# First token tiles ahead of the first two weight tiles in a hybrid encoder layer

## The chip, the cores and the metric

The kernel runs on one core of a Trainium2 chip. The time is that of one execution on the device, in microseconds; the median of several runs is given, and one further execution was taken by the hardware profiler.

## What is computed

One layer of a bidirectional encoder on 1024 tokens of width 1024, in float32. The reference, cut to its steps:

```python
h = rms_norm(x, g_mix_pre)
proj = h @ w_in                       # 1024 x 2832
aq, ak, av, dqkv, dgate, dalpha, dbeta = split(proj)
attn_o = window_attention(rope(aq), rope(ak), av, sink)          # 8 heads, +-128 tokens
dn_o = gated_deltanet(dqkv, dgate, dalpha, dbeta, conv_w, ...)   # 4 heads, both directions
x = x + rms_norm(concat(attn_o, dn_o) @ w_out, g_mix_post)
c = cross_attention(rms_norm(x, g_cross_pre), rms_norm(mem, g_mem), w_cq, w_ckv, w_co)
x = x + rms_norm(c, g_cross_post)
f = (silu(hn @ w_gate) * (hn @ w_up)) @ w_down                   # hn = rms_norm(x, g_ffn_pre)
return x + rms_norm(f, g_ffn_post)
```

The DeltaNet part sends its q, k and v columns through a short convolution of five taps, then solves small triangular systems for chunks of tokens and carries a state along the sequence in both directions.

## The kernel before

Tokens are handled in tiles of 128 (eight tiles, `NT`), the width in eight slices of 128 (`KT`). A large product is made from three: each operand is split into a high part (a rounding cast on ScalarE, line 102) and a low part (the difference, line 103), and high x high, high x low and low x high are added up in PSUM. `split` does both steps. The low part is taken on VectorE unless another engine is named.

`load_w` (line 118) fetches a weight tile of 128 columns, 512 KB, with a DMA from SyncE (line 122) and splits it into `whi` and `wlo`. Its pool `wp` holds two raw tiles (`wraw`) and two of each part, so the third weight tile is loaded when the first raw tile has been split.

The start of the kernel brings the tokens in. For each of the eight token tiles: a DMA of 512 KB into `xt`; ScalarE squares it and sums up (line 214, `junk`, `ss`); GpSimd makes the factor from the sum (`rstd_of`, lines 157 and 158, `rs`); VectorE multiplies by this factor and by the gain `gmix` (line 217); TensorE turns the tile by eight 128x128 transposes against `ident` (line 222); and `split` makes `hhi` and `hlo` of each half of it. The tiles stand in a ring of six buffers (`bufs=6`). Four tiles make one half of the sequence, `hT[0]` or `hT[1]`, and a product needs a whole half.

The first products (line 292) are those of head 0's k and q columns: two weight tiles, `ws`, against both halves. Their results go through `conv` (lines 269 to 281): ScalarE copies them out of PSUM, VectorE does four taps (line 279).

Then follow ORDER_1 (the other DeltaNet projections, `prep`, the inverse of the small blocks), ORDER_2 (gates, the further levels of the inverse, value, key and query projections of the attention, and first windows `W`) and ORDER_3, the scan stage:

```python
ORDER_3 = ("M " + "s01 W K " * 5 + "s01 K K K K " * 2 + "s01 K s01 K K").split()
```

`M` normalises the memory tokens, `s01` is one step of the two scans, which load `kv` and `pz` (lines 765 and 766) and do small products (line 757); `W` works on two windows of the attention, which load `vr`, `kr` and `qr` (lines 604 to 607), make scores (line 627), turn the weights (line 650), split them into `ph` and `pl` and multiply by the values (line 655); `K` makes one column tile of the memory's keys or values (lines 885 to 896). At the end, `ol` is normalised (line 832) and turned (line 837), and the mixer's output `d_mix` is read back in `mraw` and split into `b` for the product with `w_out` (line 976). After that come the cross-attention and the FFN.

The order of the instructions on each engine is not that of the source. A planner simulates the whole program's course and puts each engine's instructions in a queue by their due times and priorities; `tc.high_priority(AHEAD)` moves a weight's loading and splitting ahead. Each engine then works through its queue in order. All DMAs are issued from SyncE's queue.

In the program before, the loads stand on SyncE in this order: the two weight tiles, `ident`, the first token tile, `gmix`, five more token tiles, then small tables with the third and fourth weight tiles between them, then the last two token tiles. On VectorE both `wlo` stand ahead of the first line 217.

Of the kernel before, what the change touches and what calls it, by code (L numbers as in the profile page):

```python
# [10 lines left out]
F32 = mybir.dt.float32  # L11
# [8 lines left out]
P = 128  # L20
S = 1024
D = 1024
KT = D // P
# [52 lines left out]
def tile_hybrid_block(  # L76
# [4 lines left out]
    g_ffn_pre, w_gate_up, w_down, g_ffn_post, consts, out, dump=None, stop=None,  # L81
):
    nc = tc.nc
    x, mem, out = x[0], mem[0], out[0]
# [3 lines left out]
    if dump is None:  # L88
        def dump(name, ap):
            pass  # L90
# [8 lines left out]
    def split(hi, lo, src, scale=None, eng=None):  # L99

        if scale is None:
            nc.scalar.copy(hi, src)  # L102
            (eng or nc.vector).tensor_tensor(lo, src, f32(hi), ALU.subtract)  # L103
        else:
            nc.scalar.activation(hi, src, AF.Identity, scale=scale)
            nc.vector.scalar_tensor_tensor(lo, src, scale, f32(hi), ALU.mult, ALU.subtract)

    def pool(name, bufs, **kw):
        return tc.tile_pool(name=name, bufs=bufs, reuse_waits="tile", **kw)
# [5 lines left out]
    dram = ctx.enter_context(tc.tile_pool(name="dram", bufs=1, space=DRAM))  # L115
    wp = ctx.enter_context(pool("wp", 2))

    def load_w(src, k, n, eng=None):

        with tc.high_priority(AHEAD):  # L120
            raw = wp.tile([P, k, n], F32, tag="wraw", name="wraw")
            nc.sync.dma_start(raw, src.rearrange("(k p) n -> p k n", p=P))
            hi = wp.tile([P, k, n], F32R, tag="whi", name="whi")
            lo = wp.tile([P, k, n], F32R, tag="wlo", name="wlo")
            split(hi, lo, raw, eng=eng)
        return hi, lo


    ident = cst.tile([P, P], F32, name="ident")
    nc.sync.dma_start(ident, consts[:, 0:P])  # L130
    mhalf = cst.tile([P, 16], F32, name="mhalf")
    nc.gpsimd.memset(mhalf, -0.5)
    cols = cst.tile([P, P], F32, name="cols")
# [20 lines left out]
    def rstd_of(rs, ss, n, eps):  # L154

        w = ss.shape[-1]
        nc.gpsimd.tensor_scalar(rs, ss, n, eps, ALU.mult, ALU.add)
        nc.gpsimd.tensor_tensor(rs, rs, mhalf[:, :w], ALU.pow)  # L158
# [34 lines left out]
    t1 = pa1.enter_context(pool("t1a", 2, side="right"))  # L193

    def small():
        return ps.tile([P, 512], F32, tag="ps", name="ps")


    xts = [t1.tile([P, D], F32, tag="xt", name="xt", bufs=6) for _ in range(2)]
    nc.sync.dma_start(xts[0], x[0:P, :])  # L200
    gmix = t1.tile([P, D], F32, tag="gmix", name="gmix", bufs=1)
    nc.sync.dma_start(gmix, g_mix_pre[0].partition_broadcast(P))
    hT = []
    for hf in range(2):
        hi = hx.tile([P, KT, HALF], F32R, name=f"hhi{hf}")
        lo = hx.tile([P, KT, HALF], F32R, name=f"hlo{hf}")
        for j in range(4):
            t = 4 * hf + j
            xt = xts[t] if t < 2 else t1.tile([P, D], F32, tag="xt", name="xt", bufs=6)
            if t:  # L210
                nc.sync.dma_start(xt, x[t * P:(t + 1) * P, :])
            junk = t1.tile([P, D], F32, tag="junk", name="junk", bufs=1)
            ss = t1.tile([P, 1], F32, tag="ss", name="ss", bufs=4)
            nc.scalar.activation(junk, xt, AF.Square, accum_out=ss)
            rs = t1.tile([P, 1], F32, tag="rs", name="rs", bufs=4)
            rstd_of(rs, ss, 1.0 / D, EPS)
            nc.vector.scalar_tensor_tensor(xt, xt, rs, gmix, ALU.mult, ALU.mult)
            for kq in range(2):
                pt = small()
                for k in range(4):  # L220
                    c = (4 * kq + k) * P
                    nc.tensor.transpose(pt[:, k * P:(k + 1) * P], xt[:, c:c + P], ident)
                o = slice(4 * kq, 4 * kq + 4), slice(j * P, (j + 1) * P)
                split(hi[:, o[0], o[1]], lo[:, o[0], o[1]], pt.rearrange("p (k t) -> p k t", k=4))
        hT.append((hi, lo))
        dump(f"hT{hf}", (hi, lo))
# [30 lines left out]
    def proj(src_cols, eng=None):  # L257
        whi, wlo = load_w(src_cols, KT, P, eng)
        pp = [pg.tile([P, 512], F32, tag="pg", name="pg") for _ in range(2)]
        gemm_b(whi, wlo, hT, pp)  # L260
        return pp
# [21 lines left out]
    def dcols(i, h):  # L283
        return w_in[:, 768 + (4 * i + h) * P:768 + (4 * i + h + 1) * P]


    ws = [load_w(dcols(i, 0), KT, P) for i in (1, 0)]
    pps = [[None, None], [None, None]]
    for hf in range(2):
        for i in range(2):  # L290
# [4 lines left out]
    t1 = pa1.enter_context(pool("t1b", 1, side="right"))  # L295
# [581 lines left out]
    def next_kv():  # L877

        ct = kv_done[0]
        kv_done[0] += 1  # L880
        whi, wlo = load_w(w_ckv[:, ct * P:(ct + 1) * P], KT, P, nc.gpsimd)
        pp = pc.tile([P, 512], F32, tag="pc", name="pck")[:, 0:ML]
        for k in range(KT):
            for i, (w, a) in enumerate(((whi, 0), (whi, 1), (wlo, 0))):
                nc.tensor.matmul(pp, w[:, k, :], mT[a][:, k, :], start=(k == 0 and i == 0), stop=(k == KT - 1 and i == 2))
        cv = mk.tile([P, ML], F32, tag="cv", name="cv", bufs=2)
        nc.scalar.copy(cv, pp)
        if ct < KT:
            nc.sync.dma_start(d_mk[ct * P:(ct + 1) * P, :], cv)
            return  # L890
        pt = pc.tile([P, 512], F32, tag="pc", name="ptv")[:, 0:ML]
        for t in range(2):
            nc.tensor.transpose(pt[:, t * P:(t + 1) * P], cv[:, t * P:(t + 1) * P], ident)
        vv = mk.tile([P, 2, P], F32, tag="vv", name="vv", bufs=2)
        nc.scalar.copy(vv, pt.rearrange("p (t n) -> p t n", t=2))
        nc.sync.dma_start(d_mv[:, :, (ct - KT) * P:(ct - KT + 1) * P].rearrange("t p n -> p t n"), vv)
# [116 lines left out]
    for hf in range(2):  # L1013
        for kp in range(4):
            k2 = slice(2 * kp, 2 * kp + 2)
            raw = raw01 if hf == 0 and kp < 2 else raws[hf]
# [83 lines left out]
    raw = tr.tile([P, KT, HALF], F32, name="xraw")  # L1100
# [24 lines left out]
    for k in range(HK):  # L1125
        p0, p1 = turned_k(xn, k), turned_k(xn, k + HK)
        g0, g1 = gain("ffn", k), gain("ffn", k + HK)
        x12, t1, t2_, t3_ = (tr.tile([P, HALF], F32, name=f"r{i}", tag=f"r{i}") for i in range(4))
# [57 lines left out]
    ws = LA.enter_context(pool("ws", 2, side="right"))  # L1186
# [179 lines left out]
```

## Time and profile before

| | |
|---|---|
| median of 3 runs | 1670.23 us (1670.08 to 1673.58) |
| profiled execution | 1670.74 us |
| its span, first to last instruction | 1669.0 us |
| mean granted clock of TensorE | 0.975 |
| TensorE busy | 1569.7 us, 94% of the span |
| VectorE, ScalarE, GpSimd busy | 926.9, 752.5, 655.2 us |

The profile has one row for an engine, a line of the kernel and an operation: when it started, how long it took, what it wrote and read, and in brackets how long the engine had sat idle before it and what ended that. PE is TensorE's matmul side and PEld its weight loads, DVE is VectorE, ACT ScalarE, POOL GpSimd, SP SyncE, SPq its queue of DMAs. A row of the windows gives the length of a stretch, the busy time of PE, PEld, DVE, ACT and POOL with their counts, the granted share of TensorE's clock, the share of time that the DMA engines were busy, and GB/s. A row of the waits gives who waited for whom, the total in us, how often, and the longest.

### The profile page before, as it was taken

Reading aid. Unit: us, or ns where it says so; the run is one execution under the profiler, and the core shown is the slowest. Engines: PE = TensorE matmul, PEld = TensorE weight load, DVE = VectorE, ACT = ScalarE, POOL = GpSimd, SP = SyncE. Lnnn points to the kernel's source line nnn. Section 1 sums busy time; section 2 is a strip of 40 time slices with the busy share of each in tenths; the row PEclk is TensorE's granted clock in tenths of the full one; section 3 lists DMA queues with packets and bytes.
Section 4 is the critical chain, followed back from the end, with each engine's and each line's share of the span. In section 5 each row is a group of like instructions: output and inputs, shape, how many; then the busy total and the mean of one; then the engine's idle time right before and its main releaser. Section 6 shows DMA issues by size and latency. Waiting matters only on the chain.

```text
span 1669.0 us, 21742 instructions
## 1 busy us (share of the span) xinstructions
PE 1569.7 (94%) x7802; PEld 1314.5 (79%) x7802; DVE 926.9 (56%) x1407; ACT 752.5 (45%) x1528; POOL 655.2 (39%) x557
## 2 busy tenths in 40 slices
PE   6989889997999879899999999999999999999998
PEld 5878778886888767678888777788888888888886
DVE  6754987876776543453335348677544554335342
ACT  6555553246867754554335555233323332445221
POOL 2467552344437534664225340334333332321010
PEclk9999999897999999999999999999999999999999
DMA  5134256665998456354222164343222223566452
GB/s 197 40 113 139 85 164 174 164 172 159 322 313 268 111 161 235 126 177 151 76 64 99 60 208 134 119 126 102 76 76 82 88 92 105 192 203 209 137 166 77
DMA packets 275560, 240.49 MB, mean 144 GB/s; under 512 B 43240, under 2 KB 226941, under 8 KB 275453
## 3 DMA queue, kind: packets, MB, share of 16 engines
q1 hardware_dynamic: 275453, 239.11, 46.0%
q8 instruction: 61, 1.00, 0.3%
q14 instruction: 46, 0.38, 0.1%
HBM read 177.69 MB, written 58.75 MB: 142 GB/s over the span
## 4 chain that ended last, share of the span: by engine, by line
PE 53%; POOL 3%; DMA 2%; DVE 2%; issue 2%; ACT 1%; SPq 0%; POOLq 0%; ACTq 0%
PE pd L1320 7%; PE pd L1295 7%; PE pD L1149 7%; PE pE L1149 7%; PE pA L1149 7%; PE pmg L976 6%; PE pcq L254 5%; PE pB L1149 3%; PE pco L1084 1%; PE pcs L1058 1%; POOL wlo L103 1%; DMA d_mv<-vv 1%; DMA mraw<-d_mix 1%; POOL prs L158 0%; POOL pr L158 0%
## 5 line engine op out<-in xcount | busy, mean ns | idle before, releaser
L103 POOL TENSOR_TENSOR wlo<-wraw,whi 128x1024 fp32r<-128x1024 f32 x88 | 217.5, 2473 | 294.8 <-ACT whi L102 281.5
L102 ACT CAST whi<-wraw 128x1024 fp32r<-128x1024 f32 x108 | 113.4, 1050 | 170.1 <-issue 74.9
L254 PE MATMUL pg<-hhi,whi 128*128 128x512 f32 x352 | 143.2, 408 | 0.0
L254 PE MATMUL pg<-hhi,wlo 128*128 128x512 f32 x352 | 142.1, 404 | 0.0
L254 PE MATMUL pg<-hlo,whi 128*128 128x512 f32 x352 | 142.1, 404 | 0.0
L976 PE MATMUL pmg<-whi,b 128*128 128x512 f32 x384 | 117.1, 400 | 7.4 <-ACT whi L102 5.2
L1149 PE MATMUL pA<-b,whi 128*128 128x512 f32 x352 | 111.2, 398 | 3.6 <-ACT m L1166 3.1
L279 DVE SCALAR_TENSOR_TENSOR acc<-cp,cols,acc 128x1024 f32<-128x1024 f32 x48 | 77.4, 1614 | 35.0 <-ACT acc L277 34.3
L1226 POOL TENSOR_TENSOR act<-act,up 128x512 f32<-128x512 f32 x33 | 47.8, 1449 | 114.5 <-issue 63.1
L976 PEld LDWEIGHTS pmg<-whi,b 128*128 128x128 f32 x384 | 73.3, 193 | 23.7 <-ACT whi L102 5.6
L1149 PEld LDWEIGHTS pA<-b,whi 128*128 128x128 f32 x352 | 66.4, 191 | 18.6 <-ACT m L1166 4.4
L254 PEld LDWEIGHTS pg<-hhi,wlo 128*128 128x128 f32 x352 | 68.4, 194 | 13.8
L254 PEld LDWEIGHTS pg<-hhi,whi 128*128 128x128 f32 x352 | 68.4, 195 | 13.5 <-ACT hhi L102 0.2
L254 PEld LDWEIGHTS pg<-hlo,whi 128*128 128x128 f32 x352 | 68.3, 194 | 13.4
L1198 POOL TENSOR_TENSOR sr<-wraw 128x512 f32<-128x512 f32 x22 | 28.5, 1297 | 115.9 <-DMA wraw<-in_w_gate_up_dram 107.3
L976 PE MATMUL pmg<-wlo,b 128*128 128x512 f32 x192 | 70.1, 395 | 1.3 <-POOL wlo L103 1.3
L1149 PE MATMUL pA<-b,wlo 128*128 128x512 f32 x176 | 69.6, 397 | 0.0
L1320 PE MATMUL pd<-wdh,ath 128*128 128x512 f32 x176 | 69.5, 395 | 0.0
L1320 PE MATMUL pd<-wdh,atl 128*128 128x512 f32 x176 | 69.5, 395 | 0.0
L1320 PE MATMUL pd<-wdl,ath 128*128 128x512 f32 x176 | 69.5, 395 | 0.0
L1295 PE MATMUL pd<-dl,whi 128*128 128x512 f32 x176 | 68.5, 389 | 0.0
L1295 PE MATMUL pd<-dh,wlo 128*128 128x512 f32 x176 | 68.4, 389 | 0.0
(392 smaller groups left out, 4222.1 us busy)
## 6 DMA issues: line engine op xcount, KB each, us to landing
wraw<-in_w_gate_up_dram SPq DMA_DIRECT2D x52, 512.0 KB, 4.0
kv<-d_kv SPq DMA_DIRECT2D x32, 512.0 KB, 6.2
wraw<-in_w_in_dram SPq DMA_DIRECT2D x22, 512.0 KB, 4.1
araw<-d_act SPq DMA_DIRECT2D x22, 512.0 KB, 3.4
draw<-in_w_down_dram SPq DMA_DIRECT2D x22, 512.0 KB, 4.4
atr<-d_act SPq DMA_DIRECT2D x16, 704.0 KB, 4.7
d_act<-act SPq DMA_DIRECT2D x40, 256.0 KB, 2.7
d_kv<-kv SPq DMA_DIRECT2D x8, 1024.0 KB, 6.3
```

Source lines behind the costliest of these rows:

```text
L102: nc.scalar.copy(hi, src)
L103: (eng or nc.vector).tensor_tensor(lo, src, f32(hi), ALU.subtract)
L254: nc.tensor.matmul(p_, w[:, k, :], ah[a][:, k, :], start=(k == 0 and i == 0), stop=(k == nk - 1 and i == 2))
L279: nc.vector.scalar_tensor_tensor(acc, cp[:, t:t + S], taps[t], acc, ALU.mult, ALU.add)
L976: nc.tensor.matmul(pp[t], act[a][:, k, tt], w_[:, kk, :], start=(k == 0 and i == 0), stop=(k == KT - 1 and i == 2))
L1058: nc.tensor.matmul(pp[:, t2_, :], q[a][:, ct, tt], kr_[b_][:, ct, :], start=(j == 0 and i == 0), stop=(j == 1 and i == 2))
L1084: nc.tensor.matmul(po, vr_[a][:, kt, cs], pts[kt][b_], start=(kt == 0 and i == 0), stop=(kt == 1 and i == 2))
L1149: nc.tensor.matmul(out_, w[a][:, k, :], xx[b_][:, k, :], start=(start and k == 0 and i == 0), stop=(k == HK - 1 and i == 2), skip_group_ch ...
L1198: nc.gpsimd.tensor_tensor(s[0], b_[:, 0:HK], b_[:, HK:], ALU.add)
L1226: nc.gpsimd.tensor_tensor(o_, o_, up, ALU.mult)
L1295: nc.tensor.matmul(pps[t], a[:, tt], b_, start=(f == 0 and i == 0), stop=(f == NF - 1 and i == 2))
L1320: nc.tensor.matmul(pp, a[:, f - f0], b_[:, f], start=(f == 0 and i == 0), stop=(f == NF - 1 and i == 2))
```

## The change

The tiles of the first six token tiles are made at once and their loads are issued in a row, with `gmix` and `ident` after the first. The first two weight tiles are tied into this row: `load_w` takes an argument `after`, and with it the weight's DMA is planned right behind the named DMA. The weight of k goes behind the second token tile, that of q behind the fourth. `issue_after` sets an order in the queue, not a wait for the data. The computation is the same.

```diff
-    def load_w(src, k, n, eng=None):
+    def load_w(src, k, n, eng=None, after=None):
...
-            nc.sync.dma_start(raw, src.rearrange("(k p) n -> p k n", p=P))
+            with ExitStack() as order_:
+                if after:
+                    order_.enter_context(tc.issue_after(after.ins))
+                nc.sync.dma_start(raw, src.rearrange("(k p) n -> p k n", p=P))
...
     ident = cst.tile([P, P], F32, name="ident")
-    nc.sync.dma_start(ident, consts[:, 0:P])
...
-    xts = [t1.tile([P, D], F32, tag="xt", name="xt", bufs=6) for _ in range(2)]
-    nc.sync.dma_start(xts[0], x[0:P, :])
+    xts = [t1.tile([P, D], F32, tag="xt", name="xt", bufs=6) for _ in range(6)]
     gmix = t1.tile([P, D], F32, tag="gmix", name="gmix", bufs=1)
-    nc.sync.dma_start(gmix, g_mix_pre[0].partition_broadcast(P))
+    xload = []
+    for t in range(6):
+        xload.append(nc.sync.dma_start(xts[t], x[t * P:(t + 1) * P, :]))
+        if t == 0:
+            nc.sync.dma_start(gmix, g_mix_pre[0].partition_broadcast(P))
+            nc.sync.dma_start(ident, consts[:, 0:P])
...
-            xt = xts[t] if t < 2 else t1.tile([P, D], F32, tag="xt", name="xt", bufs=6)
-            if t:
+            xt = xts[t] if t < 6 else t1.tile([P, D], F32, tag="xt", name="xt", bufs=6)
+            if t >= 6:
                 nc.sync.dma_start(xt, x[t * P:(t + 1) * P, :])
...
-    ws = [load_w(dcols(i, 0), KT, P) for i in (1, 0)]
+    ws = [load_w(dcols(i, 0), KT, P, after=xload[t]) for i, t in ((1, 1), (0, 3))]
```

In the built program the queues differ in two places. At the start, SyncE has the first token tile, `gmix`, `ident`, the second, a weight, the third and fourth, a weight, the fifth and sixth; the seventh comes ahead of the third weight tile, the eighth between the third and the fourth. VectorE and ScalarE have the splits of the two weights between their steps for the token tiles, and TensorE, whose first 69 products and transposes stand as before, has some of those behind them exchanged. Then the queues are equal, instruction by instruction, until the scan stage, whose instructions are the same but stand in another order on every engine. From the product with `w_out` on they are almost equal again, and the FFN is unchanged.

## The prediction

> **What bounds the kernel now.** I read the page's head first, then the waits of the first 60 us, then the windows of the start.
>
> ```profile
> span 1669.0 us, 21742 instructions
> ...
> PE 1569.7 (94%) x7802; PEld 1314.5 (79%) x7802; DVE 926.9 (56%) x1407; ACT 752.5 (45%) x1528; POOL 655.2 (39%) x557
> ...
> PE ps L222 <- DVE xt L217: 12.8, 3, 11.7
> ...
> 0.00:12.00 12.00, 0.27 (x1) 0.27 (x2) 3.74 (x3) 5.67 (x7) 1.96 (x18) 1.00 0.88 295
> 12.00:24.00 12.00, 10.87 (x48) 8.92 (x48) 10.94 (x15) 9.82 (x19) 7.01 (x10) 1.00 0.94 310
> 24.00:60.00 36.00, 36.00 (x173) 29.40 (x171) 29.89 (x41) 19.05 (x30) 7.03 (x8) 1.00 0.20 56
> ```
>
> The window rows give busy us of PE, PEld, DVE, ACT and POOL in turn. PE is the bound: 94% of the span. Its longest single wait is the first, 11.7 us for the first scaled token tile (`xt`, L217). From 12 to 24 us it does transposes with DVE as busy as itself (10.94 of 12 us), and from 24 us it is full for 36 us. So the number that counts at the start is when PE's dense stretch begins; what it gains there is handed on, since PE's order is the same in both programs up to the scan stage (about 415 us) but for places exchanged inside the first products.
>
> The timeline of the start shows the chain. First SyncE and ScalarE:
>
> ```profile
> 0.79 1.07 SPq L122 DMA_DIRECT2D wraw<-in_w_in_dram  x2
> 3.07 0.43 SPq L200 DMA_DIRECT2D xt<-in_x_dram  x1
> 4.82 1.04 ACT L102 CAST whi<-wraw 128x1024 fp32r<-128x1024 f32 x1 [2.75 <-DMA wraw<-in_w_in_dram]
> 6.63 1.04 ACT L102 CAST whi<-wraw 128x1024 fp32r<-128x1024 f32 x1 [0.77 <-DMA wraw<-in_w_in_dram]
> 8.20 1.06 ACT L214 ACTIVATE junk<-xt 128x1024 f32<-128x1024 f32 x1 [0.52 <-DMA xt<-in_x_dram]
> 10.84 1.06 ACT L214 ACTIVATE junk<-xt 128x1024 f32<-128x1024 f32 x1 [1.49 <-DMA xt<-in_x_dram]
> ...
> 19.89 0.58 ACT L102 CAST hhi<-ps 128x512 fp32r<-128x512 f32 x1 [0.34 <-PE ps L222]
> ```
>
> Each of the first four starts when its tile lands. So a weight tile takes 1.81 us on the bus (6.63 - 4.82); gmix and the second token tile together take 2.64 (10.84 - 8.20), 1.32 each; ident and the first token tile take 1.57, ident 0.25. Then VectorE and TensorE:
>
> ```profile
> 5.89 1.23 DVE L103 TENSOR_TENSOR wlo<-wraw,whi 128x1024 fp32r<-128x1024 f32 x1 [5.89 <-ACT whi L102]
> 7.71 1.23 DVE L103 TENSOR_TENSOR wlo<-wraw,whi 128x1024 fp32r<-128x1024 f32 x1 [0.58 <-ACT whi L102]
> 10.39 1.28 DVE L217 SCALAR_TENSOR_TENSOR xt<-xt,rs,gmix 128x1024 f32<-128x1024 f32 x1 [1.46 <-POOL rs L158]
> 12.94 1.28 DVE L217 SCALAR_TENSOR_TENSOR xt<-xt,rs,gmix 128x1024 f32<-128x1024 f32 x1 [1.26 <-DMA rows<-in_g_mem_dram]
> 14.14 0.69 DVE L103 TENSOR_TENSOR hlo<-ps,hhi 128x512 fp32r<-128x512 f32 x1
> 14.94 1.28 DVE L217 SCALAR_TENSOR_TENSOR xt<-xt,rs,gmix 128x1024 f32<-128x1024 f32 x1
> ...
> 17.34 1.28 DVE L217 SCALAR_TENSOR_TENSOR xt<-xt,rs,gmix 128x1024 f32<-128x1024 f32 x1
> 18.54 0.69 DVE L103 TENSOR_TENSOR hlo<-ps,hhi 128x512 fp32r<-128x512 f32 x1
> 19.14 1.28 DVE L217 SCALAR_TENSOR_TENSOR xt<-xt,rs,gmix 128x1024 f32<-128x1024 f32 x1
> 20.33 0.22 DVE L240 CAST mU_r<-CE 128x128 fp32r<-128x128 f32 x1
> ...
> 21.20 1.28 DVE L217 SCALAR_TENSOR_TENSOR xt<-xt,rs,gmix 128x1024 f32<-128x1024 f32 x1
> ...
> 11.73 1.97 PE L222 MATMUL ps<-ident,xt 128*128 128x128 f32 x8 [11.73 <-DVE xt L217]
> 18.77 1.94 PE L222 MATMUL ps<-ident,xt 128*128 128x128 f32 x8 [0.52 <-DVE xt L217]
> 20.53 1.22 PE L254 MATMUL pg<-hhi,whi 128*128 128x512 f32 x2
> 21.55 2.84 PE L222 MATMUL ps<-ident,xt 128*128 128x128 f32 x16
> 24.14 0.48 PE L254 MATMUL pg<-hlo,whi 128*128 128x512 f32 x1
> ```
>
> Both weight subtractions (`wlo`) are over at 8.94 us, before the first `xt` can start: they are hidden by the wait for tokens. After 12.94 VectorE has no gap, one `xt` step per 1.20 us and one `hlo` step per 0.60 (start to start). The dense stretch begins at 24.14, after the transposes of the sixth tile.
>
> **The change part by part.** *Loads.* The queue becomes x0, gmix, ident, x1, w, x2, x3, w, x4, x5. With the bus times above x0 lands at 4.82 - (1.81 - 1.32) = 4.33 us instead of 8.20, gmix 5.65, ident 5.90, x1 7.22 instead of 10.84, first weight 9.03, x2 10.35, x3 11.67, second weight 13.48, x4 14.80, x5 16.12. The bytes up to x5 are the same. The third and fourth weight loads move back, behind the seventh and eighth token tile, and `wab` and the positions stand behind them on SyncE. Their cover is long: PE is full until 60 us with the first two weights and what follows in order, so I price this at nothing; if the cover is gone, one tile late costs 1.81.
>
> *The token chain.* Tile landed to `xt` started took 2.19 us for the first tile (8.20 to 10.39) and 2.10 for the second. So the first `xt` starts at 6.52, 3.87 earlier, and the second at 9.32, 3.62 earlier. That is the head start.
>
> *What eats it.* In the changed program's order VectorE does xt, xt, hlo, wlo, hlo, xt, hlo, xt, hlo, wlo, hlo, xt, mU, mL, hlo, xt: both `wlo` now stand between token steps, and one `hlo` more stands ahead of the sixth `xt`. From the second `xt` to the start of the sixth there are four `xt` steps (4.80), six `hlo` (3.60), two `wlo` (1.20 each by the step of the like-sized `xt`, 2.40) and the two small casts (20.33 to 20.60, 0.27): 11.07 us, where before 8.26 passed (12.94 to 21.20). Add 0.40 because the third `xt` waits: ScalarE runs the cast of the first weight (1.04) and the second `hhi` between the squares, so the third square starts at about 11.2 and its `xt` 2.10 later, at 13.3 instead of 12.9. The sixth `xt` then starts at 9.32 + 11.07 + 0.40 = 20.8 instead of 21.20: 0.4 us earlier. Of 3.62 us some 3.2 are gone.
>
> *PE behind it.* The first two products (20.53) wait for the seventh `hhi`, on ScalarE at 19.89. Now ScalarE does there, in order, the second weight's cast (from 14.6), square, `hhi`, square, `hhi`, `hhi`: 1.04 + 2 x 1.15 + 2 x 0.58 = 4.5, so the seventh starts at about 19.1, 0.8 earlier. The dense stretch follows the later of the two, the sixth tile: 0.4 us earlier, with 0.0 to 0.8 as bounds.
>
> *PE's clock.* Eight transposes took 1.97 and 1.94 us until 20.5 us, and later 1.04:
>
> ```profile
> 31.76 1.04 PE L222 MATMUL ps<-ident,xt 128*128 128x128 f32 x8
> ```
>
> So PE runs at half speed at first, and the sixteen in 2.84 us at 21.55 show the change in their midst, about 23 us. Where it falls in the changed kernel no row shows. If it keeps its place against PE's start of work, nothing changes. [...]
>
> *A neighbour.* GpSimd's power in `rstd_of` took 0.55 us at 16.36 and 1.60 at 17.42, while an `xt` ran:
>
> ```profile
> 16.36 0.55 POOL L158 TENSOR_TENSOR rs<-rs,mhalf 128x1 f32<-128x1 f32 x1
> 17.42 1.60 POOL L158 TENSOR_TENSOR rs<-rs,mhalf 128x1 f32<-128x1 f32 x1
> ```
>
> If `wlo` holds it up too, as much as 1.05 us once may fall on the path: the start's lower bound becomes -0.65. [...]
>
> *The scan stage.* Because the order is planned for the whole program, the change also reorders all five queues between about 415 and 630 us, where window attention, the scan steps and the memory keys share PE; the instructions are the same. Before and after it (ORDER_1, ORDER_2, the output products, the FFN) every queue stands as it was. PE's waits there, the longest of the first kind, and what stood ahead of it on ScalarE:
>
> ```profile
> PE pow L655 <- ACT ph L102: 10.9, 9, 3.0
> PE ptv L893 <- ACT cv L887: 6.7, 4, 3.0
> PE psc L837 <- DVE ol L832: 5.0, 1, 5.0
> ...
> PE psc L757 <- DMA pz<-d_pz: 0.3, 1, 0.3
> ...
> 485.15 0.50 PE L655 MATMUL pow<-ph,vhi 128*128 128x512 f32 x1 [2.81 <-ACT ph L102]
> ...
> 482.04 0.40 ACT L615 CAST vhi<-vr 128x256 fp32r<-128x256 f32 x1 [4.52 <-DMA vr<-d_v]
> 483.97 0.51 ACT L610 CAST khi<-kr 128x384 fp32r<-128x384 f32 x1 [1.53 <-DMA kr<-d_k]
> ...
> 600.00:620.00 20.00, 11.94 (x86) 11.15 (x84) 10.03 (x16) 7.94 (x25) 6.44 (x5) 0.83 0.54 157
> ```
>
> The last three memory values have no other PE work between product and transpose in either order, and the last `ol` (L832) stands behind two `b` subtractions in both: those waits stay. What can move is the 10.9 us for `ph`. The new order has as many places where `ph` stands behind a cast of a freshly loaded tile, so I take 0. Bounds: half of the 10.9 saved or as much added, 5.5 us each way (estimate).
>
> *Sum.* 0.4 at the start, 0 in the scan stage: the profiled 1670.74 (span 1669.0 and 1.7 around it) becomes 1670.3. That execution lies 0.5 above the median of the runs, 1670.23, so the forecast for a median is 1669.8.
>
> **The rivals.** A difference of 0.2%, 3.3 us, is about what a measurement of this kernel can tell from no change.
>
> *The head start comes through.* If VectorE found room for the two `wlo` in the gap before its second `xt`, PE would keep the 3.62 us: 1666.6. Against it: the order puts the first `wlo` behind that `xt`, and the first weight lands only at 9.03.
>
> *The scan stage waits less.* In the new SyncE order the window loads (L607, L604, L605) often stand ahead of scan loads (L765, L766) that they stood behind. If the stall of 2.81 at 485.15 goes that way, and with it a stretch of half clock, the gain is 2.81 + 1.7 (the 600:620 slice lost 0.17 x 20 = 3.4 us of clock around its idle time; half of it for one stall, an estimate): 1669.8 - 4.5 = 1665.3.
>
> *The scan stage waits more: slower.* The same move puts the scan's own loads later. A scan step's product needs its `kv` and `pz`; a load that comes after its turn stops PE, whose queue is in order, with window and memory products behind it. It decides once one load is later than the step before it covers, and one more stall like the longest costs the same 4.5 us: 1674.3. For it: the slack of a scan load is known for the old order alone. Against it: PE waited for such a load only 0.3 us.
>
> **How the numbers follow.** Forecast (within 3.3 us) 0.47; head start through 0.07 and scan stage better 0.18, together faster 0.25; scan stage worse 0.28, a little above its mirror image, because the scan steps are the stage's longest serial chain and their loads are the ones that moved back. The range is 1669.8 less 5.5, 1664.3, to 1669.8 plus 5.5 and the 1.0 of the neighbour, 1676.3; what is left out are two or more stalls of one sign.
>
> **What would show it.** Right: the first transposes at about 8.0 us instead of 11.73, the two `wlo` at about 11 and 17 us between token steps with hardly a gap on VectorE, and the product that stood at 24.14 between 23.3 and 24.2; then windows to 400 us that hold the same busy time, and the rest of the difference between 415 and 630 us. Wrong at the start: a dense stretch that begins before 22 us (VectorE was not full) or after 25 (clock, or GpSimd held). Wrong in the scan stage: more than 5.5 us of changed PE waits there, for `ph`, `kv` or `pz`.

## The result, and the profile after

| | before | changed |
|---|---|---|
| median of 14 runs each | 1671.07 us | 1666.24 us |
| range of the runs | 1668.72 to 1675.18 | 1661.09 to 1669.80 |
| profiled execution | 1670.74 | 1669.54 |

The ratio is 0.9971, with a 95% interval of 0.9961 to 0.9981: the changed kernel is faster by 0.29%, 4.8 us, a little more than the 3.3 us that the prediction called no change. The forecast of 1669.8 was the case "no change", and it did not come true; the range of 1664.3 to 1676.3 holds the time, and the rival "the scan stage waits less" had named 1665.3. Ratios leave out executions far above the others of their program: one of 2071.14 us at a granted clock of 0.70 (run e9 below) and one of 4480.20 us (e5).

The profiled execution of the changed kernel lies 3.3 us above its own median, so the two profiles differ by 1.2 us where the medians differ by 4.8. A single pair of profiles doesn't carry the difference; the experiments below do.

*The start.* This is the timeline of the changed kernel, with the same columns as before. Because of the added lines, L222 is now L228, L217 is L223, L254 is L260 and L214 is L220.

```profile
4.37 1.06 ACT L220 ACTIVATE junk<-xt 128x1024 f32<-128x1024 f32 x1 [2.30 <-DMA xt<-in_x_dram]
6.81 1.29 DVE L223 SCALAR_TENSOR_TENSOR xt<-xt,rs,gmix 128x1024 f32<-128x1024 f32 x1 [6.81 <-DMA gmix<-in_g_mix_pre_dram]
8.15 1.97 PE L228 MATMUL ps<-ident,xt 128*128 128x128 f32 x8 [8.15 <-DVE xt L223]
8.39 1.06 ACT L220 ACTIVATE junk<-xt 128x1024 f32<-128x1024 f32 x1 [2.87 <-DMA xt<-in_x_dram]
10.49 1.28 DVE L223 SCALAR_TENSOR_TENSOR xt<-xt,rs,gmix 128x1024 f32<-128x1024 f32 x1 [2.39 <-POOL rs L160]
...
12.29 1.22 DVE L103 TENSOR_TENSOR wlo<-wraw,whi 128x1024 fp32r<-128x1024 f32 x1
...
18.03 1.21 DVE L103 TENSOR_TENSOR wlo<-wraw,whi 128x1024 fp32r<-128x1024 f32 x1
...
21.19 4.00 PE L228 MATMUL ps<-ident,xt 128*128 128x128 f32 x16 [0.44 <-DVE xt L223]
...
21.83 1.27 DVE L223 SCALAR_TENSOR_TENSOR xt<-xt,rs,gmix 128x1024 f32<-128x1024 f32 x1
...
24.84 0.74 PE L260 MATMUL pg<-hlo,whi 128*128 128x512 f32 x1
```

The first token tile lands at 4.37 us, as worked out (4.33), and the first transposes begin at 8.15. But `gmix` and the second tile are late: 6.81 and 8.39 where 5.65 and 7.22 had been worked out. VectorE is then full from 10.49 to the sixth `xt` at 21.83, and the product that stood at 24.14 stands at 24.84. The head start at the first tile is 3.6 us (8.15 instead of 11.73), and nothing of it is left at the product.

*The scan stage.* These are PE's waits between 410 and 665 us in the changed kernel (L655 is now L661, L893 is L899, L837 is L843). The columns are the total, how often, and the longest:

```profile
PE ptv L899 <- ACT cv L893: 7.2, 3, 3.9
PE psc L843 <- DVE ol L838: 4.2, 1, 4.2
PE pow L661 <- ACT ph L102: 3.6, 5, 1.7
PE psw L633 <- DVE m L635: 3.5, 5, 0.7
PE psc L763 <- DMA pz<-d_pz: 1.7, 1, 1.7
PE psc L763 <- DVE kv L784: 1.7, 1, 1.7
PE pow L661 <- DVE pl L103: 1.1, 5, 0.2
```

The waits for `ph` fell from 10.9 to 3.6 us. New are 1.7 for `kv` (a step of VectorE, L784, not a load), 1.4 more for `pz` and 1.0 more for `m`. The waits for `cv` and `ol` at the end, which the prediction said would stay, are 7.2 and 4.2 where they were 6.7 and 5.0.

To compare whole stages over many profiles, take two TensorE instructions that stand at the same place of the queue in every program: the last product of the second `psc<-kv,pz` group of the scan stage, and one product with `w_out` (the 1927th and the 3407th on TensorE). In before, and below it in the changed kernel, they lie in these rows:

```profile
423.10 1.16 PE L757 MATMUL psc<-kv,pz 128*128 128x128 f32 x8
...
662.95 0.39 PE L976 MATMUL pmg<-wlo,b 128*128 128x512 f32 x1
```

```profile
422.60 1.13 PE L763 MATMUL psc<-kv,pz 128*128 128x128 f32 x8 [0.56 <-DVE mT L106]
...
659.97 0.62 PE L982 MATMUL pmg<-wlo,b 128*128 128x512 f32 x2
```

The eighth product of the first row begins at 423.99 in before, so its stage is 662.95 - 423.99 = 238.96 us. In the changed kernel it begins at 423.45 and the other, the second of its row, at 660.20: 236.75 us. "The stage" below is always this stretch, and "the arrival" is the time of its first instruction.

### The profile page after: what moved, and what is told of

The parts are those of the page before. It is cut to its first block, busy times and chain, and to the rows that moved or that the text cites. A ratio compares the mean times of both kernels' runs of the same rounds, so it can differ in the third digit from the quotient of the medians.

```text
span 1667.8 us, 21742 instructions
## 1 busy us (share of the span) xinstructions
PE 1570.1 (94%) x7802; PEld 1313.7 (79%) x7802; DVE 931.9 (56%) x1407; ACT 751.9 (45%) x1528; POOL 654.3 (39%) x557
## 4 chain that ended last, share of the span: by engine, by line
PE 65%; DVE 9%; DMA 5%; POOL 4%; issue 4%; ACT 3%; SPq 1%; POOLq 0%; ACTq 0%; DVEq 0%
PE pd L1326 7%; PE pd L1301 7%; PE pD L1155 7%; PE pE L1155 7%; PE pA L1155 7%; PE pmg L982 6%; PE pcq L260 5%; PE pB L1155 3%; PE pg L260 3%; PE psc L763 3%; PE pow L661 1%; PE pco L1090 1%; DVE acc L285 1%; DVE A L512 1%; PE pcs L1064 1%
## 5 line engine op out<-in xcount | busy, mean ns | idle before, releaser
L260 PE MATMUL pg<-hhi,whi 128*128 128x512 f32 x352 | 142.4, 406 | 0.0
L260 PE MATMUL pg<-hhi,wlo 128*128 128x512 f32 x352 | 141.9, 403 | 0.0
L260 PE MATMUL pg<-hlo,whi 128*128 128x512 f32 x352 | 141.5, 403 | 0.0
L260 PEld LDWEIGHTS pg<-hhi,wlo 128*128 128x128 f32 x352 | 68.1, 194 | 13.6
L260 PEld LDWEIGHTS pg<-hhi,whi 128*128 128x128 f32 x352 | 68.1, 194 | 13.4 <-ACT hhi L102 0.3
L260 PEld LDWEIGHTS pg<-hlo,whi 128*128 128x128 f32 x352 | 68.0, 193 | 13.4
```

The lines of the kernel that those rows point to most:

```text
L260: nc.tensor.matmul(p_, w[:, k, :], ah[a][:, k, :], start=(k == 0 and i == 0), stop=(k == nk - 1 and i == 2))
```

## The experiments

The theory was that the gain is made in the scan stage, by the order that the planner chose anew; the rivals were the start (the token tiles that come first) and chance (which stretches of half clock a run happens to draw: from 310 to 323 us the granted clock was 0.50 all through in the profile of before, and 0.87 on average in that of the changed kernel). The first four runs cross two starts with two orders of the scan stage. To hold an order, a kernel is given a table of the instruction names of each engine's queue from the scan stage on, taken from the other program, and ties each instruction behind the one before it (the code is cut to its steps):

```diff
+def in_this_order(tc, nc):
+    at = {i.name: i for i in nc.cur_bb.bb.instructions}
+    for names in SCAN_ORDER.values():          # one list for each engine
+        for a, b in zip(names, names[1:]):
+            tc.add_manual_dep(at[b], a, NO_SYNC, reason="scan order")
...
         tile_hybrid_block(tc, *args)
+        in_this_order(tc, nc)
```

Such an edge sets an order in a queue and adds no wait for data. Before the stage each program keeps its own order. The tables hold no score step of VectorE (`sc`, line 629), so these stand where the planner puts them.

**e1: the changed kernel again.**

> The changed kernel itself once more. Scan-order theory (the gain is made where the planner put the scan stage, 415 to 630 us, in another order) and start theory (the gain is made by the token tiles that come first) both expect the 4.8 us again: ratio 0.996 to 0.998 against the kernel before. [...] In the profile the dense products should again begin near 24.8 us, with the product that stood at 24.14 us before; if that place wanders by more than 1 us between two profiles of one program, the start cannot be read from one profile.

**e2: old start, new order of the scan stage** (before, with the changed kernel's table).

> The kernel before, its loads untouched, but with every queue tied from the scan stage on to the order that the changed kernel has there. Scan-order theory: 4.8 us faster than before, ratio 0.996 to 0.998, and the wait of 2.81 us for ph at 485 us gone. Start theory: within 0.001 of 1. Chance theory: within 0.002 of 1.

**e3: new start, old order** (the changed kernel, with before's table).

> The changed kernel with the new loads and the new start, but with every queue tied from the scan stage on to the order of the kernel before. Scan-order theory: no gain, ratio 0.999 to 1.001, and by the profiled start, where the dense products began 0.7 us later, rather 0.5 us slower. Start theory: the whole 4.8 us, ratio 0.996 to 0.998. Chance theory: within 0.002 of 1.

**e4: only the first token tile's load ahead of the weights.**

```diff
-    ws = [load_w(dcols(i, 0), KT, P, after=xload[t]) for i, t in ((1, 1), (0, 3))]
+    ws = [load_w(dcols(i, 0), KT, P, after=xload[t]) for i, t in ((1, 0), (0, 0))]
```

> Only the load of the first token tile goes ahead of the two weights, and ident behind gmix; every other instruction on every queue stands as before, the scan stage too. The second tile still lands behind both weights, so all theories expect within 0.001 of 1; the first transposes may start a few us earlier, but the third tile's stay near 17 us. It shows what a measurement of an indifferent change looks like.

Each row has one profile for its last four columns; "PE idle" is the stage less TensorE's busy time in it, "clock" the mean granted share of TensorE's clock there.

| | start | scan order | ratio to before, 95% interval | arrival | stage | PE idle | clock |
|---|---|---|---|---|---|---|---|
| before | old | old | 1 | 423.99 | 238.96 | 26.9 | 0.97 |
| e4 | x0 first only | old | 0.9986 (0.9972 to 1.0001) | 427.64 | 238.87 | 23.7 | 0.96 |
| e3 | new | old | 1.0010 (0.9998 to 1.0023) | 424.04 | 242.93 | 25.1 | 0.94 |
| e2 | old | new | 0.9981 (0.9966 to 0.9996) | 426.61 | 235.91 | 22.5 | 0.97 |
| e1 | new | new | 0.9969 (0.9958 to 0.9981) | 423.93 | 237.31 | 20.7 | 0.96 |
| the changed kernel | new | new | 0.9971 (0.9961 to 0.9981) | 423.45 | 236.75 | 22.8 | 0.97 |

The gain goes with the order of the scan stage. The order changes the ratio by -0.0019 with the old start and by -0.0041 with the new one, on average -0.0030 or 5.0 us; the start changes it by +0.0010 with the old order and by -0.0012 with the new one, on average nothing. The stage takes 238.87 to 242.93 us in the old order and 235.91 to 237.31 in the new; the two groups do not overlap, with three profiles each. The arrival is no earlier with the new start (423.45 to 424.04) than in before (423.99); in further profiles with the old start it lies on both sides (422.45 to 426.61 in e2, e5, e6 and e12). Chance is out as the cause: e1 repeats the 0.997, and e3, with the same start, has 1.0010. But e4, which should be indifferent, measured 0.9986 with an interval that just reaches 1, so a difference of 0.0015 is not to be read as one, and the 0.0019 of e2 alone would say little.

A part of the gain comes with TensorE's clock. The stage of e3 is the longest of the six at the lowest clock, 0.94, though TensorE idles no longer in it than in before: its 242.93 is clock, not waits. The idle time is 25.3 us on average in the old order and 22.0 in the new, 3.3 less. Over whole executions the mean granted clock was 0.9743, 0.9746 and 0.9728 in before, e4 and e3, and 0.9753 and 0.9750 in e2 and e1. A thousandth of some 1670 us is 1.7 us, so about 2 of the 5.0 us may be clock (an estimate from these means). Whether it is the shorter waits that leave TensorE a higher clock was not tried.

The waits for `ph` go with the order as well. This is the line of PE's waits in e3, with the old order, and then that in e2, with the new one:

```profile
PE pow L661 <- ACT ph L102: 9.3, 7, 3.5
```

```profile
PE pow L655 <- ACT ph L102: 5.7, 6, 2.5
```

In e2 one wait of 2.5 us is left, so the expectation that the wait near 485 us goes did not come true there; in the changed kernel 1.7 is left of it. What is gone in both is the other long one, near 576 us, to which this section comes back.

**Which queue does it?** The prediction's rival had named SyncE's: window loads ahead of scan loads. e5 gives the kernel before the new order on SyncE alone, e6 on the four engines alone.

> The kernel before, with only SyncE's queue tied to the changed kernel's order from the scan stage on; TensorE, VectorE, ScalarE and GpSimd keep the old order there. Load theory (window loads that stand ahead of the scan loads land earlier, so the casts in front of ph do not hold ScalarE): TensorE's waits for ph fall from 9 to 11 us to 2 to 6, the waits of the cast of vr for its DMA (6.5 us in all before) go, ratio about 0.998. Queue theory (the gain is where ph and the casts stand on ScalarE and TensorE): ph waits stay at 9 to 11 us, ratio 0.999 to 1.001, or slower where loads now stand in an order that no engine takes them in.

> The mirror of it: the four engines in the changed kernel's order from the scan stage on, SyncE's loads in the old order, the old start. Load theory: ph waits stay at 9 to 11 us, ratio 0.999 to 1.001. Queue theory: ph waits 2 to 6 us, ratio about 0.998. If both orders are needed together, this run and the one before are each within 0.001 of 1, or slower.

e5 came out at 1.0205 (1.0183 to 1.0227) and a stage of 271.82 us, e6 at 1.0017 (1.0003 to 1.0031) and 244.08 us. Neither half gains; the new loads with the old engines lose 2%. These are ScalarE's longest wait in e5 (8.9 us in before) and, after it, two of PE's:

```profile
ACT khi L610 <- DMA kr<-d_k: 39.9, 7, 10.7
```

```profile
PE pow L655 <- ACT ph L102: 13.2, 8, 3.1
PE ptv L893 <- ACT cv L887: 12.1, 4, 6.7
```

So the load theory is wrong: in e5 the loads that the new order puts ahead stand in the wrong place for the old order of the engines. In e6, with the old loads, the `ph` waits are short (4.7 us), as the queue theory has it, but the time is not: other waits, such as 1.4 us for `khi`, come in. In both runs a load order beside the other order of the engines cost time.

**The place of `ph`.** What stands ahead of the late `ph` on ScalarE can be read off the timeline. These are ScalarE's rows before, ahead of the longest wait for `ph`, and then PE's:

```profile
572.73 0.62 ACT L644 ACTIVATE sc<-sc,es 128x384 f32<-128x384 f32 x1 [0.16 <-DVE es L642]
...
574.00 1.62 ACT L644 ACTIVATE sc<-sc,es 128x384 f32<-128x384 f32 x3
575.65 1.07 ACT L102 CAST ph<-ptw 128x512 fp32r<-128x512 f32 x2
```

```profile
576.29 0.79 PE L655 MATMUL pow<-ph,vhi 128*128 128x512 f32 x1 [2.99 <-ACT ph L102]
```

And the same two in the changed kernel:

```profile
574.62 1.08 ACT L102 CAST ph<-ptw 128x512 fp32r<-128x512 f32 x2
...
576.53 2.14 ACT L650 ACTIVATE sc<-sc,es 128x384 f32<-128x384 f32 x4
```

```profile
575.26 0.49 PE L661 MATMUL pow<-ph,vhi 128*128 128x512 f32 x1 [0.16 <-ACT ph L102]
```

The old order scales the next window's weights (four instructions, with two copies among them; 2.14 us in the changed kernel's row) and then casts the `ph` that PE stands waiting for; the new order has the two the other way round, and PE's wait is 0.16 instead of 2.99. e9 makes this exchange and two like it by hand in the old order (the cast and the copy in front of the squares stayed, unlike what the expectation says). All five tables are otherwise those of before. A further execution of the same kernel, e12, gives its profile. In it two score steps of VectorE, which no table holds, also stand earlier than in before (at 488.98 and 577.33 us); PE's waits for them, the line for `m`, are 2.5 us in both profiles. The list is written out in short, with the times of before in brackets:

```diff
 # ScalarE's list in the table of before
+ph(484.51)                       # moved up
 vhi(482.04) khi(483.97)          # casts that wait for the DMAs of vr and kr
-ph(484.51)
...
+ph(532.10)                       # moved up
 osq osq osq osq
-ph(532.10)
...
 vhi
-sc(572.73)
 ao ao
+ph(575.65) ph(576.13)            # moved up
+sc(572.73)
 sc sc sc
-ph(575.65) ph(576.13)
```

> The kernel before, all queues tied to their own order from the scan stage on, except that on ScalarE four casts of ph stand earlier: the one at 484.51 us ahead of the casts of vr and kr that waited for their DMAs, the two at 575.65 ahead of the four scalings of the next window's weights (2.14 us), the one at 532.10 ahead of four squares of ol and the cast and copy in front of them. Place theory (the waits for ph are made by what stands ahead of ph on ScalarE): 2.2 of the 2.81, most of the 2.99 and about 0.9 of the 1.00 us of waits go, so the ph waits fall from 9 to 11 us to 4 to 5 and the stage between 424 and 663 us from 239 to 243 us to 235 to 238; ratio 0.997 to 0.998. Bulk theory (the many other exchanges of the new order make the gain, and the ph waits only stand for them): the waits turn up behind the next instruction on ScalarE, ratio 0.999 to 1.001.

> The kernel of run e9 once more, for a profile at full clock. Place theory: the waits for ph between 410 and 665 us come to 4 to 5 us in all instead of 9 to 11, with none of over 1 us near 483 and 573, and the stage takes 235 to 238 us. Bulk theory: the ph waits have gone down no further than 9 us, or others have come in their place and the stage takes 239 us or more.

The ratio is 0.9970 (0.9960 to 0.9980): four casts in another place give as much as the whole new order. In e12 the stage takes 237.22 us, and PE's waits are these:

```profile
PE pow L655 <- ACT ph L102: 3.3, 4, 1.5
PE psw L627 <- DVE m L629: 2.5, 4, 0.7
PE pck L885 <- POOL wlo L103: 1.6, 1, 1.6
...
PE psw L627 <- POOL vlo L616: 1.2, 1, 1.2
```

The waits for `ph` fall from 10.9 to 3.3 us, below the 4 to 5 expected; waits of 1.6 and 1.2 us for GpSimd come in their place. The bulk theory falls: without the other exchanges of the new order the gain is there. The two large waits are gone, as these rows of e12 show:

```profile
482.09 0.48 PE L655 MATMUL pow<-ph,vhi 128*128 128x512 f32 x1
...
574.46 0.49 PE L655 MATMUL pow<-ph,vhi 128*128 128x512 f32 x1
```

How much of e9's gain comes through the waits themselves is not shown. In e12 TensorE idles 23.0 us in the stage, 3.9 less than in before, but the stage is only 1.7 us shorter, at a clock of 0.96 instead of 0.97. Over whole executions the mean granted clock was 0.9765 in the eleven of e9 that are counted and 0.9729 in the seventeen of before measured beside them; the difference of 0.0036 is worth up to 6 us of 1670 (an estimate), as much as the gain of 5.0.

**e10: the same by hand in the new order.** The remaining two casts of `ph` that wait behind the next window's exponentials are moved ahead of them.

> The changed kernel, all queues tied to their own order from the scan stage on, except that on ScalarE two casts of ph stand earlier: the one at 490.18 us ahead of the four exponentials of the next window, the one at 561.21 likewise. Place theory: the waits of 1.68 and 0.89 us go, together 2.6 us, ratio to before 0.995 to 0.996 where the changed kernel had 0.997. Bulk theory: 0.997, as without it.

The ratio is 0.9966 (0.9952 to 0.9979), the stage 237.20 us: no gain over the changed kernel. The expectation of the place theory missed, and the profile of e10 tells why. These are PE's wait, and then the rows of VectorE and of ScalarE ahead of it:

```profile
492.20 0.50 PE L661 MATMUL pow<-pl,vhi 128*128 128x512 f32 x1 [2.15 <-DVE pl L103]
```

```profile
491.38 0.16 DVE L647 TENSOR_TENSOR es<-es,ssum 128x4 f32<-128x4 f32 x1 [2.95 <-ACT es L646]
491.46 0.68 DVE L103 TENSOR_TENSOR pl<-ptw,ph 128x512 fp32r<-128x512 f32 x1
```

```profile
488.70 0.58 ACT L102 CAST ph<-ptw 128x512 fp32r<-128x512 f32 x1
...
491.16 0.19 ACT L646 ACTIVATE es<-es 128x4 f32<-128x4 f32 x1
```

`ph` is done early, but the next product needs `pl`, and `pl` stands on VectorE behind `es`, which needs the exponentials that `ph` was moved ahead of. The 1.68 us for `ph` became 2.15 for `pl`, and PE's waits for `pl` come to 4.7 us in all, where they were 1.1 in the changed kernel. A cast moved on ScalarE alone did not help here, because its partner on VectorE was not moved with it.

**The start by itself.** e7 moves the two `wlo` of the first weights from VectorE to GpSimd, with the new order held from the scan stage on. It is not held before: by the traces the planner has also exchanged some instructions on every queue between the start and about 420 us.

```diff
-    ws = [load_w(dcols(i, 0), KT, P, after=xload[t]) for i, t in ((1, 1), (0, 3))]
+    ws = [load_w(dcols(i, 0), KT, P, nc.gpsimd, after=xload[t]) for i, t in ((1, 1), (0, 3))]
```

> The changed kernel, its scan stage and all behind it tied to its own order, with the low parts of the first two weights on GpSimd instead of VectorE. The prediction's step that VectorE is full between the second and the sixth xt, with two wlo of 1.20 us among them: the sixth xt starts 2.4 us earlier than 21.83, at 19.4, and the dense products 2 us earlier than 24.8; the whole time then is 1 to 2 us under the changed kernel's, ratio to before 0.995 to 0.997. Rival: GpSimd takes more than the two instructions save, because the factors rs of the next tiles wait behind wlo on it (its two power steps took 0.55 to 1.60 us) or VectorE's xt is slowed beside it: dense products no earlier, ratio 0.997 to 0.998 as without it.

The timeline of e7 has these rows:

```profile
11.05 2.78 POOL L103 TENSOR_TENSOR wlo<-wraw,whi 128x1024 fp32r<-128x1024 f32 x1 [0.77 <-ACT whi L102]
...
14.77 1.28 DVE L223 SCALAR_TENSOR_TENSOR xt<-xt,rs,gmix 128x1024 f32<-128x1024 f32 x1 [1.98 <-POOL rs L160]
...
16.71 2.36 POOL L103 TENSOR_TENSOR wlo<-wraw,whi 128x1024 fp32r<-128x1024 f32 x1
17.17 2.98 DVE L223 SCALAR_TENSOR_TENSOR xt<-xt,rs,gmix 128x1024 f32<-128x1024 f32 x1
...
25.77 0.48 PE L260 MATMUL pg<-hlo,whi 128*128 128x512 f32 x1
```

At the start the rival is right, both ways: the first `wlo` on GpSimd holds up `rs` and so the third `xt` (14.77; 14.23 in the changed kernel), and beside the second one an `xt` takes 2.98 us instead of 1.28. The dense product comes at 25.77, later than before. The whole time is nevertheless the lowest measured, 1664.20 us, ratio 0.9953 (0.9937 to 0.9969). e11 adds it to e10:

> The run before with the low parts of the first two weights on GpSimd as well. If that start, which began its dense products at 25.8 us instead of 24.2 to 24.8, is worth nothing, the ratio is that of the run before within 0.001; if the 0.9953 that it measured was its own, this run is a further 0.0015 lower, near 0.994.

It measured 0.9955 (0.9941 to 0.9970), dense product at 25.16. Both intervals overlap that of the changed kernel, and the rows at the start speak for a loss, not a gain. The arrivals are 419.94 and 429.28 us, although the two programs have the same order on TensorE up to there; the mean granted clock up to the arrival was 0.97 in the first and 0.95 in the second. So a profile's arrival says little about a start. The clock may also be why e7 measured lowest: its six executions had a mean of 0.9790, before beside it 0.9736, and the difference of 0.0054 is worth up to 9 us of 1670 (an estimate), more than the 7.2 us gained. Whether this version is really 2 us better than the changed kernel, and why its clock was higher, stays open.

**e8: gmix behind the second token tile.**

```diff
-        if t == 0:
+        if t == 1:
             nc.sync.dma_start(gmix, g_mix_pre[0].partition_broadcast(P))
             nc.sync.dma_start(ident, consts[:, 0:P])
```

> One look at the start alone: the changed kernel with gmix and ident behind the second token tile (the first weight then comes ahead of gmix), the scan stage tied to the changed kernel's order. In the changed kernel's profile the DMA engines moved only 239 GB/s between 4 and 6 us, with gmix and ident in flight, and x1 landed 1.2 us later than the prediction had it. If gmix or ident is slow to load early, x1 now lands at 4.33 + 1.32 = about 5.7 us and the low rate moves to where gmix stands, 7 to 9 us. If the bus is slow in these first microseconds whatever it carries, x1 lands at 6.2 to 6.9 and the low rate stays between 4 and 6 us.

The windows of the changed kernel, then of e8; the last columns are the DMA share and GB/s:

```profile
4.00:6.00 2.00, 0.00 (x0) 0.00 (x0) 0.00 (x0) 1.15 (x2) 0.22 (x2) 1.00 0.97 239
6.00:8.00 2.00, 0.00 (x0) 0.00 (x0) 1.19 (x1) 0.00 (x0) 0.53 (x1) 1.00 1.02 365
```

```profile
4.00:6.00 2.00, 0.00 (x0) 0.00 (x0) 0.00 (x0) 1.15 (x2) 0.01 (x1) 1.00 1.05 373
6.00:8.00 2.00, 0.00 (x0) 0.00 (x0) 0.00 (x0) 1.42 (x3) 1.33 (x4) 1.00 0.98 317
```

And from the timeline of e8, the square of the second tile:

```profile
6.08 1.06 ACT L220 ACTIVATE junk<-xt 128x1024 f32<-128x1024 f32 x1 [0.28 <-DMA xt<-in_x_dram]
```

The second tile lands at 6.08 us, 1.43 behind the first (4.65), against 4.02 with `gmix` and `ident` between them. The time lies between the two that were expected. The rate at 4 to 6 us is against the second theory, since the bus carried 373 GB/s there without `gmix` and `ident`. The first theory came true in part: the low rate did move, but where the two stand now, behind the first weight (7.73), the windows have 317 and, from 8 to 10 us, 367 GB/s, not 239. So the two were slow in the changed kernel's place and less so later. Which of them it is, and why the bus carried 408 GB/s at 8 to 10 us in before, where `gmix` stood among the loads, was not tried. The whole of this one execution took 1671.06 us, which is too little to place it.

## Why the prediction was right or wrong

- **The loads: sum right for the first tile, mis-sized for `gmix`, `ident` and the second tile.** 4.33 worked out, 4.37 measured; but the three that follow took 4.02 us where 7.22 - 4.33 = 2.89 had been taken from the bus time of other loads. That is the whole 1.17 us by which the second `xt` was late (9.32 worked out, 10.49 measured). The price of a transfer was taken from where it stood in the old order.
- **What eats the head start: right.** From the second to the sixth `xt` 11.07 + 0.40 = 11.47 us were worked out, and 21.83 - 10.49 = 11.34 passed. The two `wlo` stand between the token steps (12.29 and 18.03) and VectorE has hardly a gap. The neighbour term came, but off the path: GpSimd's first step for `rs`, 0.19 us at 9.63, took 0.79 at 12.77 beside a `wlo`, and the third `xt` (14.23) followed an `hlo` without a gap.
- **PE behind it: near.** The dense product was put between 23.3 and 24.2; in four profiles with the new start it stood at 24.07 (e10), 24.18 (e1), 24.61 (e3) and 24.84, and in five with the old start between 23.98 (e12) and 24.37 (e5). So the start is worth nothing or a little loss, not 0.4 gained. By the whole times, too, no effect of the start is seen (-0.0001 on average of +0.0010 and -0.0012).
- **PE's clock: rightly left open.** The same program had its transposes at 21.19 at half speed in one execution (sixteen in 4.00 us, above) and at full speed in another, e1:

```profile
21.19 1.07 PE L228 MATMUL ps<-ident,xt 128*128 128x128 f32 x8 [0.47 <-DVE xt L223]
```

  The first transposes began at 8.15 us in the one and at 8.62 in e1, so the step to full speed did not keep its place against PE's start of work: in e1 it had come by 12.57 us after that start (21.19 - 8.62), in the other execution not yet by 16.69 us after it (24.84 - 8.15), where a product took 0.74 us that took 0.48 in e1.
- **The scan stage: the step that failed.** "The new order has as many places where `ph` stands behind a cast of a freshly loaded tile, so I take 0." The count looked for one kind of neighbour only. The longest wait, 2.99 us at 576.29, came from another: the scalings of the next window's weights. Reading ScalarE's rows ahead of each of the longest waits, and then the same places in the new order, would have shown the exchange. The stage took on average 240.25 us in the old order (before, e3, e4) and 236.66 in the new (the changed kernel, e1, e2): 3.6 us, inside the bound of 5.5 that the prediction gave for the time; it is this bound that keeps the measured time in the range, not the 0 that was taken. The waits for `ph` alone changed by 7.3, from 10.9 in before to 3.6 in the changed kernel (9.3 in e3 with the old order, 5.7 in e2 and 1.8 in e1 with the new), which by the prediction's own mark (more than 5.5 us of changed waits) shows the step wrong.
- **The rival "the scan stage waits less": right in the stage, wrong in mechanism, its price met by luck.** It named 4.5 us, from the stall of 2.81 us at 485.15 and a stretch of half clock. But 1.68 of that stall stayed; the largest single fall, from 2.99 to 0.16, came near 576 us. It gave SyncE's order as the cause, and SyncE's order alone cost 2% (e5). The place of four `ph` casts on ScalarE is enough (e9). That the clock goes with the waits, as the rival had it, fits the means of whole executions above, but is not shown.
- **The rival "the scan stage waits more": its waits stayed small.** The load of `pz` cost 1.4 us more, against 7.3 us less for `ph`, and this does not go with the order: the wait is 1.2 us in e3, with the old order, and 1.0 in e1, with the new. The 1.7 us for `kv` are a wait for VectorE's step on it; the profile's list of PE's waits has none for the load of `kv`.
- **The chances.** "Faster" had 0.25, and "no change" 0.47. With two bounds of 5.5 us either way and no reason found for zero, the middle had no right to be the likeliest by so much.

## What to carry to other kernels

Where a planner orders the queues of the whole program, a change at the start may act 400 us later, and more there than at its own place. Compare the orders of the queues before pricing the edit, and for each of the longest waits of the bottleneck engine read what stands ahead of the awaited instruction on its own queue, in the old order and in the new. Then hold one order and vary the other part: with two starts and two orders, four programs showed where the gain is made, which no pair of profiles could. Put the granted clock beside each time before reading a difference of a few us.

## What the runs showed that was not expected

- The order of a few instructions on an engine that is far from full decides. ScalarE was busy 752 us of 1669, yet four casts in another place on it gave 0.3% (e9).
- An order of loads that belongs to another order of the engines cost 2% (e5: 39.9 us of ScalarE waiting for `kr`), far more than either whole order differs from the other.
- With a 512 KB broadcast of one row and a 64 KB table in flight the bus moved 239 GB/s at 4 to 6 us, and 373 with the second token tile and the first weight in their place (e8).
- Two programs with the same order on TensorE reached the scan stage at 419.94 and 429.28 us, with a mean granted clock of 0.97 and 0.95 on the way (e7, e11).
- A `wlo` of 1.2 us on VectorE took 2.4 to 2.8 us on GpSimd, and beside it an `xt` on VectorE took 2.98 instead of 1.28 (e7).
